# Two transformer blocks on one core: reciprocals, the query's rope and the order of weight splits in latent attention

## The chip, the cores and the metric

The program runs on one core of a Trainium2 chip, as one launch. The metric is the device time in microseconds (us). Engines: TensorE (PE; matmuls and transposes), VectorE (DVE), ScalarE (ACT), GpSimd (POOL) and SyncE (SP), which here issues the weight loads. Each engine works through its own list of instructions in order; semaphores tie the lists together.

## What is computed

256 tokens of width 1024 go through two blocks. In short (`reference`):

```
first_block, layer 0:  x = x + ab_mixer(rms_norm(x))          # mLSTM heads beside a gated mixing, then @ w_out
                       x = x + relu(rms_norm(x) @ w1)**2 @ w2
             layer 1:  x = x + mla_mixer(rms_norm(x))
                       x = x + relu(rms_norm(x) @ w1)**2 @ w2
second_block:          chunked attention with a relative bias, then a SwiGLU, each with norms around it

mla_mixer:  cq, ckv, kr = split(h @ w_in, [384, 640])
            q  = rms_norm(cq) @ w_uq    # 16 heads x (64 without position + 32 rotated)
            kv = rms_norm(ckv) @ w_ukv  # 16 heads x (64 of key + 64 of value)
            rotate the 32 of each query head and the shared kr by position
            p  = softmax(q k^T * 96**-0.5);  out = (p v) @ w_out
apply_rope: [x1 cos - x2 sin, x1 sin + x2 cos]
```

The change concerns the order of the work and the way the rotation is done.

## The kernel before

**Weights and passes.** All matrix products with weights are in full fp32 accuracy by three passes of TensorE: a weight is split into `whi`, a copy rounded to the short format, and `wlo`, the rest; the activations likewise into xh and xl. A product is xh·whi (L373), xl·whi (L374) and xh·wlo (L375), all added in one PSUM tile. `Stream` brings the weights in chunks of up to 1 MB: SP loads a chunk into one of three raw buffers, ACT copies it to `whi` (L149) and DVE, for some chunks POOL, subtracts to get `wlo` (L154), in one, two or four parts; there are four buffers of each. When both halves of a chunk are done with a raw buffer, SP loads the next one. `S.get` hands a chunk to the matmuls, `S.done` lets the coming splits be issued.

**What sets the order.** Within an engine a scheduler sets the order by a timeline it works out; `hot` gives a piece of code priority. Two marks bind the splits of weights: a `wlo` on DVE may not come before the instruction kept in `S.low`, a `whi` on ACT not before the one in `S.behind`. The code sets `S.low` at DVE work that is wanted soon: the copies of qn and kn, the maxima (L1090), the copies of the transposed probabilities, and `split_x` (L302), which splits each finished residual column into xh and xl. `split_x` runs at the end of the mixer (`residual`, L499), of both FFNs (`residual_scaled`, L507, L508) and of the attention.

**Latent attention.** From the input projection (`c_evac`) come the latent ch, cl in two parts. `thin` makes the shared rotary key from the weight wkr, which ACT's queue loads into a place that the first FFN used: DVE scales it (`ws`, L363), TensorE multiplies. `colsum` (L323) adds the squares of the residual on TensorE for the norm; the last sum before it is on DVE (L318). After the values v, `q_rope` makes two of four rotary query tiles: 18 matmuls, a copy to SBUF on ACT (L1000), a shuffle of halves on DVE (L1002), the cosine product on POOL (L1003), the sine product (L1004) and the sum (L1005) on DVE. `q_nope` (18 matmuls, a copy to qn, L1008) and `k_nope` (12 matmuls, kn, L1013) make the rest for one of four groups of four heads. For each group `sc` writes the scores into four PSUM tiles (L1074 for the part without position, L1079 for the rotary part) and `exps` reads them: maxima on DVE (L1089, L1090), eight exponentials on ACT (L1093) that also sum. `nrm` takes reciprocals of the sums (DVE, L1100) and multiplies the probabilities (DVE and POOL, L1103), `tr` transposes them on TensorE (L1117) and copies them to pT (L1122), `pv` multiplies by v (L1132) and splits the result into yh and yl (L1142, L1143), `c_out` is the output projection. TensorE's order in this stage is that of the code. Matmul results rotate through four PSUM tiles (`mm`), scores through four others (`aux`).

## Time and profile before

| | |
|---|---|
| Time, three runs | 898.32, 900.12, 904.68 us; median 900.12 |
| Profiled execution | 897.51 us; its span 895.8 us |
| Busy | TensorE 865.6 us (97%), DVE 573.8 (64%), ACT 469.6 (52%), POOL 268.5 (30%) |
| Mean granted clock of TensorE | 0.990 of full |
| Stages (us of the span) | the mixer's last sums with the residual at 134, the first FFN's at 308, first scores of the attention at 342 |

The profile is of one execution. Its span runs from the first to the last instruction; 1.7 us of the execution's time lie around it. A timeline row gives the start, the duration, the engine, the line of the kernel, the operation and what it writes from what; "x4" means that four like instructions are merged, and the bracket tells how long the engine had been idle before it and what ended the idle. A merged row's duration is that of the whole.

### The profile page before, as it was taken

To read this page: it belongs to the slowest core of one execution; us is meant where nothing else is said; L and a number is where in the kernel's file an instruction comes from. 1 tells how busy PE (TensorE), PEld (TensorE's weight loads), DVE (VectorE), ACT (ScalarE), POOL (GpSimd) and SP (SyncE) were. 2 spreads that over 40 slices of the span, in tenths; PEclk is the share of its full clock that TensorE was granted. 3 is DMA by queue.
4 is the path that set the end of the run, shared out by engine and by line. 5 is a ranking of instruction groups with operands and counts; after the bars stand their busy time and mean duration, and the time that the engine had idled before them with its cause. 6 is when DMAs were issued, how large, how long until landed. Compare 5 with 4: busy or idle time off the path is not lost.

```text
span 895.8 us, 16451 instructions
## 1 busy us (share of the span) xinstructions
PE 865.6 (97%) x6744; PEld 805.2 (90%) x6744; DVE 573.8 (64%) x921; ACT 469.6 (52%) x824; POOL 268.5 (30%) x281
## 2 busy tenths in 40 slices
PE   8899989999999997799999999999999999999996
PEld 6788989999999996589999999999867799999885
DVE  7698768755355658846855456658873776666442
ACT  6676545855444363545655544515476664455331
POOL 6877713333100443375433212320156000000000
PEclk9999999999999999999999999999999999999999
DMA  8543427655455532223755455569424465555511
GB/s 288 215 146 137 141 79 257 218 201 194 142 190 188 194 130 95 95 94 102 277 193 201 170 183 194 190 204 304 154 94 142 165 235 192 194 197 202 185 67 48
DMA packets 25579, 154.38 MB, mean 172 GB/s; under 512 B 2736, under 2 KB 5216, under 8 KB 8224
## 3 DMA queue, kind: packets, MB, share of 16 engines
q1 hardware_dynamic: 22176, 148.18, 46.8%
q10 hardware_dynamic: 3040, 4.36, 2.0%
q8 instruction: 53, 0.87, 0.4%
q0 software_dynamic: 288, 0.79, 0.3%
q14 instruction: 22, 0.18, 0.1%
HBM read 152.25 MB, written 1.07 MB: 171 GB/s over the span
## 4 chain that ended last, share of the span: by engine, by line
PE 83%; DVE 8%; ACT 3%; issue 2%; DMA 2%; POOL 0%; SPq 0%; DVEq 0%; POOLq 0%; ACTq 0%
PE mm L373 20%; PE mm L375 20%; PE mm L374 20%; PE aux L472 2%; PE aux L471 2%; PE aux L470 2%; PE mm L435 2%; DVE acc L717 2%; DVE wlo L154 2%; PE mm L437 2%; PE mm L436 2%; ACT whi L149 1%; ACT pr L1093 1%; PE aux L1074 1%; PE mm L470 1%
## 5 line engine op out<-in xcount | busy, mean ns | idle before, releaser
L149 ACT ACTIVATE whi<-raw 128x1024 fp32r<-128x1024 f32 (+2 forms) x318 | 285.3, 951 | 225.7 <-PE mm L374 140.2
L154 DVE TENSOR_TENSOR wlo<-raw,whi 128x1024 fp32r<-128x1024 f32 (+2 forms) x254 | 307.4, 1251 | 80.1 <-ACT whi L149 80.0
L373 PE MATMUL mm<-xh,whi 128*128 128x256 f32 x1080 | 300.3, 279 | 0.2 <-DVE head L499 0.2
L374 PE MATMUL mm<-xl,whi 128*128 128x256 f32 x1080 | 299.0, 277 | 0.0
L375 PE MATMUL mm<-xh,wlo 128*128 128x256 f32 x1080 | 298.6, 277 | 0.0
L373 PEld LDWEIGHTS mm<-xh,whi 128*128 128x128 f32 x1080 | 203.0, 189 | 1.0 <-issue 0.8
L374 PEld LDWEIGHTS mm<-xl,whi 128*128 128x128 f32 x1080 | 203.6, 189 | 0.2
L375 PEld LDWEIGHTS mm<-xh,wlo 128*128 128x128 f32 x1080 | 203.5, 189 | 0.0
L373 PE MATMUL mm<-hh,whi 128*128 128x256 f32 x512 | 141.3, 276 | 0.0
L374 PE MATMUL mm<-hl,whi 128*128 128x256 f32 x512 | 141.3, 276 | 0.0
L375 PE MATMUL mm<-hh,wlo 128*128 128x256 f32 x512 | 141.3, 276 | 0.0
L373 PEld LDWEIGHTS mm<-hh,whi 128*128 128x128 f32 x512 | 96.1, 188 | 0.0
L374 PEld LDWEIGHTS mm<-hl,whi 128*128 128x128 f32 x512 | 96.1, 188 | 0.0
L375 PEld LDWEIGHTS mm<-hh,wlo 128*128 128x128 f32 x512 | 96.1, 188 | 0.0
L524 POOL TENSOR_TENSOR fu<-ft 128x512 f32<-128x512 f32 (+1 forms) x36 | 55.2, 1536 | 116.5 <-ACT ft L522 111.8
L154 POOL TENSOR_TENSOR wlo<-raw,whi 128x512 fp32r<-128x512 f32 (+2 forms) x64 | 81.8, 1305 | 21.2 <-ACT whi L149 21.1
L318 POOL TENSOR_TENSOR s_acc<-s_acc,sq 128x256 f32<-128x256 f32 x37 | 40.4, 1098 | 147.8 <-ACT sq L317 147.1
L1229 POOL TENSOR_TENSOR r<-v,nhalf 128x1 f32<-128x1 f32 x4 | 2.2, 558 | 193.5 <-DVE v L1228 193.5
L435 PE MATMUL mm<-whi,xh 128*128 128x512 f32 x96 | 38.7, 420 | 1.3 <-ACT whi L149 1.3
L436 PE MATMUL mm<-wlo,xh 128*128 128x512 f32 x96 | 37.9, 398 | 1.7 <-DVE wlo L154 1.7
L437 PE MATMUL mm<-whi,xl 128*128 128x512 f32 x96 | 37.7, 396 | 0.6 <-DVE xl L1438 0.6
L525 DVE TENSOR_TENSOR hl<-fu,hh 128x512 fp32r<-128x512 f32 (+1 forms) x36 | 23.3, 650 | 22.4 <-POOL fu L524 22.4
(371 smaller groups left out, 1314.4 us busy)
## 6 DMA issues: line engine op xcount, KB each, us to landing
raw<-in_w_dram SPq DMA_DIRECT2D x64, 1024.0 KB, 5.0
raw<-in_w_gu_dram SPq DMA_DIRECT2D x22, 1024.0 KB, 4.8
raw<-in_w_qk_dram SPq DMA_DIRECT2D x12, 1024.0 KB, 4.9
raw<-in_w_down_dram SPq DMA_DIRECT2D x11, 1024.0 KB, 4.9
raw<-in_w_ab_out_dram SPq DMA_DIRECT2D x4, 1024.0 KB, 5.0
raw<-in_w_c_out_dram SPq DMA_DIRECT2D x4, 1024.0 KB, 5.1
raw<-in_w_v_dram SPq DMA_DIRECT2D x4, 1024.0 KB, 7.0
raw<-in_w_o_dram SPq DMA_DIRECT2D x4, 1024.0 KB, 4.8
```

The lines of the kernel that those rows point to most:

```text
L149: self.nc.scalar.activation(hi[:, s], r[:, s], AF.Copy)
L154: eng.tensor_tensor(lo[:, s], r[:, s], hi[:, s].bitcast(F32), op=ALU.subtract)
L318: state["sum"] = (dve if k == last else pool).tensor_tensor(acc, acc, sq, op=ALU.add)
L373: pe.matmul(ps, wh, h, start=start, stop=False)
L374: pe.matmul(ps, wh, l, start=False, stop=False)
L375: pe.matmul(ps, wl, h, start=False, stop=stop)
L435: pe.matmul(pss[tt], h[k][:, ts], wh[:, s], start=k == 0, stop=False)
L436: pe.matmul(pss[tt], h[k][:, ts], wl[:, s], start=False, stop=False)
L437: pe.matmul(pss[tt], l[k][:, ts], wh[:, s], start=False, stop=k == nk - 1)
L470: pe.matmul(ps, h[k][:, ts], wh[:, ns], start=k == 0, stop=False)
L524: pool.tensor_tensor(u[:, 0:g], t[:, 0:g], t[:, 0:g], op=ALU.mult)
L525: dve.tensor_tensor(hl[:, m:m + g], u[:, 0:g], hh[:, m:m + g].bitcast(F32), op=ALU.subtract)
```

## The change

It has four parts. `split_x` no longer sets `S.low`; it keeps its instruction aside, and only the end of the attention puts it into `S.low`. The reciprocals are issued after the instruction in `S.low`. In the rotation the ACT copy goes: shuffle and cosine product read PSUM on DVE, the sine product goes to POOL, the sum stays on DVE. The second `q_rope` is moved from ahead of the first `q_nope` to between the first and second group of scores, and with it the points at which chunks are fetched and released; the second half of the query weights is fetched after the second scores. Beside these, the probabilities get 12 buffers instead of 16, and the rest of the output, yl, sets `S.low`.

```diff
--- before.py
+++ after.py
@@ -302,8 +302,8 @@
     def split_x(k, src, scale):
 
         act.activation(xh[:, k], src, AF.Copy, scale=scale)
-        S.low = dve.scalar_tensor_tensor(xl[:, k], src, scale, xh[:, k].bitcast(F32), op0=ALU.mult,
-                                         op1=ALU.subtract)
+        state["xl"] = dve.scalar_tensor_tensor(xl[:, k], src, scale, xh[:, k].bitcast(F32), op0=ALU.mult,
+                                               op1=ALU.subtract)
 
     def split_lo(k, g):
         dve.scalar_tensor_tensor(xl[:, k], x[:, k], col(g, k), xh[:, k].bitcast(F32), op0=ALU.mult,
@@ -909,6 +909,7 @@
         v = ap.tile([P, 2, D], F32, name="v")
         yh, yl = [None] * KB, [None] * KB
         pT_ = [ap.tile([P, 2, T], F32, name=f"pT{i}") for i in range(4)]
+        q2_ = ap.tile([P, 2, T], F32, name="q2")
         mp = mpc.__enter__()
         r2 = ap.tile([P, 2], F32, name="r2")
         rq = ap.tile([P, 2], F32, name="rq")
@@ -996,13 +997,11 @@
 
             ps = tiles(w, 6 * g, CK[2:5], CL[2:5], 3, 2)
             qs = qr[:, 2 * g:2 * g + 2]
-            q2 = mp.tile([P, 2, T], F32, tag="q2", name="q2")
-            act.activation(qs, ps, AF.Copy)
             for i in range(2):
-                dve.stream_shuffle(q2[:, i], qs[:, i], SHUF)
-                pool.tensor_tensor(qs[:, i], qs[:, i], cosT, op=ALU.mult)
-                dve.tensor_tensor(q2[:, i], q2[:, i], sinT, op=ALU.mult)
-                S.low = dve.tensor_tensor(qs[:, i], qs[:, i], q2[:, i], op=ALU.add)
+                dve.stream_shuffle(q2_[:, i], ps[:, i], SHUF)
+                S.low = dve.tensor_tensor(qs[:, i], ps[:, i], cosT, op=ALU.mult)
+                pool.tensor_tensor(q2_[:, i], q2_[:, i], sinT, op=ALU.mult)
+                dve.tensor_tensor(qs[:, i], qs[:, i], q2_[:, i], op=ALU.add)
 
         def q_nope(w, g):
             S.low = dve.tensor_copy(qn[g], tiles(w, 6 * (g % 2), CK[2:5], CL[2:5], 3, 2))
@@ -1051,10 +1050,8 @@
         w = S.get()
         q_rope(w, 0)
         key_rope()
-        q_rope(w, 1)
-        S.done()
-        w = S.get()
-        q_nope(w, 0)
+        wn = S.get()
+        q_nope(wn, 0)
         wk = S.get()
         k_nope(wk, 0)
         later.flush()
@@ -1084,7 +1081,7 @@
             for p in range(2):
                 mx = mp.tile([P, 2, 2], F32, tag="mx", name="mx", bufs=3)
                 sm = mp.tile([P, 2, 2], F32, tag="sm", name="sm", bufs=8)
-                prs = [mp.tile([P, 2, T], F32, tag="pr", name="pr", bufs=16) for _ in range(2)]
+                prs = [mp.tile([P, 2, T], F32, tag="pr", name="pr", bufs=12) for _ in range(2)]
                 for i in range(2):
                     dve.tensor_reduce(mx[:, i], pss[2 * p + i], axis=AX, op=ALU.max)
                 S.low = dve.tensor_tensor(mx, mx, spread(nsrq.unsqueeze(1), 1, 2), op=ALU.mult)
@@ -1097,7 +1094,8 @@
 
         def nrm(j):
             prs, sm = st_p[j]
-            dve.reciprocal(sm, sm)
+            with tc.issue_after(S.low.ins):
+                dve.reciprocal(sm, sm)
             for i in range(2):
                 for qt in range(2):
                     (pool if i else dve).tensor_scalar(prs[i][:, qt], prs[i][:, qt], sm[:, i, qt:qt + 1], None,
@@ -1140,19 +1138,19 @@
                 S.behind = act.activation(yh[j], o[:, 0:T], AF.Copy)
             else:
                 dve.tensor_copy(yh[j], o[:, 0:T])
-            dve.tensor_tensor(yl[j], o[:, 0:T], yh[j].bitcast(F32), op=ALU.subtract)
+            S.low = dve.tensor_tensor(yl[j], o[:, 0:T], yh[j].bitcast(F32), op=ALU.subtract)
 
         sc(0)
-        q_nope(w, 1)
+        q_nope(wn, 1)
+        S.done(held=3)
+        k_nope(wk, 1)
+        q_rope(w, 1)
         S.done(held=2)
-        k_nope(wk, 1)
-        w = S.get()
-        q_nope(w, 2)
         nrm(0)
         nrm(1)
         sc(1)
-        q_nope(w, 3)
-        S.done(held=2)
+        w = S.get()
+        q_nope(w, 2)
         k_nope(wk, 2)
         tr(0)
         tr(1)
@@ -1160,6 +1158,8 @@
         nrm(2)
         nrm(3)
         sc(2)
+        q_nope(w, 3)
+        S.done(held=2)
         k_nope(wk, 3)
         S.done()
         tr(2)
@@ -1201,6 +1201,7 @@
                 for k in (6, 7):
                     c_out(w, m, k)
             hot(residual, 2 * g, pss[g], s_acc[1], "ffn_norm1")
+        S.low = state["xl"]
         S.done(t=5.0)
         mctx.__exit__(None, None, None)
         mpc.__exit__(None, None, None)
```

In the rows of order below a name's number is that of its tile, and the bracket names what the instruction waits for (a load of SP's queues is DMAHW).

DVE at the end of the mixer, in the output projection (L806, L788 make its inputs; L499 adds finished tiles to the residual; wlo_1448 belongs to the last chunk of its weights). Before:

```order
L788 TENSOR_TENSOR yah_1114<-yt_1344,yah_1114 128x256 [waits Activation_49]
L499 TENSOR_TENSOR head_78<-mm_1299,head_78 128x256 [waits PE_49]
L499 TENSOR_TENSOR head_78<-mm_1306,head_78 128x256 [waits PE_49]
L499 TENSOR_TENSOR head_78<-mm_1310,head_78 128x256 [waits PE_49]
L499 TENSOR_TENSOR head_78<-mm_1314,head_78 128x256 [waits PE_49]
L305 SCALAR_TENSOR_TENSOR xl_93<-head_78,xh_92 128x256 [waits DVE_49,Activation_49] x2
L499 TENSOR_TENSOR head_78<-mm_1443,head_78 128x256 [waits PE_49]
L499 TENSOR_TENSOR head_78<-mm_1443,head_78 128x256
L305 SCALAR_TENSOR_TENSOR xl_93<-head_78,xh_92 128x256 [waits DVE_49,Activation_49] x2
L154 TENSOR_TENSOR wlo_1448<-raw_1199,whi_1447 128x1024 [waits DMAHW2_49]
L154 TENSOR_TENSOR wlo_1448<-raw_1199,whi_1447 128x1024
```

With the change, where wlo_1448 stands:

```order
L818 TENSOR_TENSOR sg_158<-mm_1221,rbc0_86 128x512 [waits PE_49]
L788 TENSOR_TENSOR ybl_153<-yt_1187,ybh_152 128x256 [waits Activation_49]
L154 TENSOR_TENSOR wlo_1448<-raw_1199,whi_1447 128x1024 [waits DMAHW2_49,Activation_49]
L806 SCALAR_TENSOR_TENSOR yt_1258<-aux_1255,head_78,sg_158 128x256 [waits DVE_49]
L154 TENSOR_TENSOR wlo_1448<-raw_1199,whi_1447 128x1024 [waits Activation_49]
L788 TENSOR_TENSOR ybl_153<-yt_1210,ybh_152 128x256 [waits Activation_49]
L788 TENSOR_TENSOR yah_1114<-yt_1258,yah_1114 128x256 [waits Activation_49]
L806 SCALAR_TENSOR_TENSOR yt_1272<-aux_1269,head_78,sg_158 128x256 [waits DVE_49]
L806 SCALAR_TENSOR_TENSOR yt_1331<-aux_1328,head_78,sg_158 128x256 [waits DVE_49,PE_49,Pool_49]
```

Both halves of wlo_1448 have moved from behind four xl and six L499 to before the last inputs of the projection; one yt (L806) stands between them, and the last ybl and all the yah (L788) behind them.

DVE at the end of the first FFN, its last column. Before:

```order
L507 TENSOR_TENSOR rs_3620<-mm_3507,rbc0_86 128x256 [waits PE_49]
L508 TENSOR_TENSOR head_78<-rs_3620,head_78 128x256 [waits DVE_49]
L318 TENSOR_TENSOR s_acc0_88<-s_acc0_88,sq_3623 128x256 [waits Activation_49,Pool_49]
L305 SCALAR_TENSOR_TENSOR xl_93<-head_78,xh_92 128x256 [waits DVE_49,Activation_49]
L363 TENSOR_TENSOR ws_3870<-wkr_3659,head_78 128x256 [waits DMAHW1_49]
```

With the change:

```order
L507 TENSOR_TENSOR rs_3620<-mm_3507,rbc0_86 128x256 [waits PE_49]
L508 TENSOR_TENSOR head_78<-rs_3620,head_78 128x256 [waits DVE_49]
L363 TENSOR_TENSOR ws_3871<-wkr_3660,head_78 128x256 [waits DMAHW1_49]
L318 TENSOR_TENSOR s_acc0_88<-s_acc0_88,sq_3623 128x256 [waits Activation_49,Pool_49]
L305 SCALAR_TENSOR_TENSOR xl_93<-head_78,xh_92 128x256 [waits DVE_49,Activation_49]
```

L363, which waits for the load of wkr, has moved ahead of the last sum of squares (L318) and of the last xl (L305).

ACT in the attention, between the values and the second chunk of query weights (whi_4021 before, whi_4092 with the change). Before:

```order
L1025 ACTIVATE v_3644<-mm_3926,rkv_3654 128x512 [waits PE_49]
L149 ACTIVATE whi_4021<-raw_3883 128x768 [waits DMAHW3_49,Pool_49]
L149 ACTIVATE whi_4021<-raw_3883 128x768
L1000 ACTIVATE qr_3642<-mm_3943 128x512 [waits PE_49]
L1000 ACTIVATE qr_3642<-mm_3984 128x512 [waits PE_49]
L1093 ACTIVATE pr_4086,sm_4085<-aux_4064,mx_4084,srq_3655 128x256 [waits DVE_49,DMAHW1_49,PE_49,Pool_49]
L1093 ACTIVATE pr_4086,sm_4085<-aux_4064,mx_4084,srq_3655 128x256
```

With the change (lines are shifted by one to three):

```order
L1024 ACTIVATE v_3644<-mm_3927,rkv_3655 128x512 [waits PE_49]
L1090 ACTIVATE pr_4048,sm_4047<-aux_4026,mx_4046,srq_3656 128x256 [waits DVE_49,DMAHW1_49,PE_49,Pool_49]
L1090 ACTIVATE pr_4048,sm_4047<-aux_4026,mx_4046,srq_3656 128x256
L1090 ACTIVATE pr_4049,sm_4047<-aux_4027,mx_4046,srq_3656 128x256 [waits PE_49]
L1090 ACTIVATE pr_4049,sm_4047<-aux_4027,mx_4046,srq_3656 128x256
L1090 ACTIVATE pr_4059,sm_4058<-aux_4028,mx_4057,srq_3656 128x256 [waits DVE_49,PE_49]
L1090 ACTIVATE pr_4059,sm_4058<-aux_4028,mx_4057,srq_3656 128x256
L1090 ACTIVATE pr_4060,sm_4058<-aux_4029,mx_4057,srq_3656 128x256 [waits PE_49]
L1090 ACTIVATE pr_4060,sm_4058<-aux_4029,mx_4057,srq_3656 128x256
L149 ACTIVATE whi_4092<-raw_3884 128x768 [waits DMAHW3_49,Activation_49]
L149 ACTIVATE whi_4092<-raw_3884 128x768
```

The copies qr are gone, and the two whi of the second query chunk have moved from ahead of the first group's exponentials to behind them.

DVE from there, behind the first group's maxima. Before:

```order
L1090 TENSOR_TENSOR mx_4084<-mx_4084,nsrq_3656 128x4 [waits DVE_49]
L1090 TENSOR_TENSOR mx_4095<-mx_4095,nsrq_3656 128x4 [waits DVE_49]
L1100 RECIPROCAL sm_4085<-sm_4085 128x4 [waits Activation_49]
L1008 COPY qn_3635<-mm_4106 128x512 [waits PE_49]
L1103 TENSOR_SCALAR pr_4086<-pr_4086,sm_4085 128x256 [waits DVE_49]
L1103 TENSOR_SCALAR pr_4086<-pr_4086,sm_4085 128x256
L1013 TENSOR_TENSOR kn_3639<-mm_4126,rbc1_87 128x256 [waits PE_49]
L1013 TENSOR_TENSOR kn_3639<-mm_4126,rbc1_87 128x256
L1100 RECIPROCAL sm_4096<-sm_4096 128x4 [waits Activation_49]
L1103 TENSOR_SCALAR pr_4097<-pr_4097,sm_4096 128x256 [waits DVE_49]
L1103 TENSOR_SCALAR pr_4097<-pr_4097,sm_4096 128x256
L154 TENSOR_TENSOR wlo_4131<-raw_3923,whi_4130 128x1024 [waits DMAHW4_49,Activation_49]
```

With the change:

```order
L1007 COPY qn_3635<-mm_4068 128x512 [waits PE_49]
L1012 TENSOR_TENSOR kn_3639<-mm_4088,rbc1_87 128x256 [waits PE_49]
L1012 TENSOR_TENSOR kn_3639<-mm_4088,rbc1_87 128x256
L154 TENSOR_TENSOR wlo_4093<-raw_3884,whi_4092 128x768 [waits DMAHW3_49,Activation_49]
L1001 STREAM_SHUFFLE q2_3649<-mm_4106 128x256 [waits PE_49]
L1002 TENSOR_TENSOR qr_3642<-mm_4106,cosT_96 128x256
L1001 STREAM_SHUFFLE q2_3649<-mm_4106 128x256
L1002 TENSOR_TENSOR qr_3642<-mm_4106,cosT_96 128x256
L1098 RECIPROCAL sm_4047<-sm_4047 128x4
L1098 RECIPROCAL sm_4058<-sm_4058 128x4
L154 TENSOR_TENSOR wlo_4093<-raw_3884,whi_4092 128x768 [waits Activation_49]
L154 TENSOR_TENSOR wlo_4169<-raw_3924,whi_4168 128x1024 [waits DMAHW4_49,Activation_49]
```

The reciprocals have moved behind the copies qn and kn of the second group, behind half a split of the second query chunk, which waits for ACT, and behind four instructions of the second rope half.

## Rows read from the trace of the kernel before

**Rows 1.** Waits of TensorE over the span: us in total, times, longest.
```profile
PE aux L1074 <- DVE kn L1013: 4.8, 2, 3.5
PE mm L375 <- DVE wlo L154: 2.4, 1, 2.4
```

**Rows 2.** Windows: us; busy us (instructions) of each engine; clock; DMA share; GB/s.
```profile
127.00:130.40 3.40, 3.40 (x17) 3.40 (x18) 3.40 (x5) 0.00 (x0) 0.00 (x0) 0.50 0.40 87
342.60:345.70 3.10, 3.10 (x16) 2.45 (x16) 3.10 (x5) 0.00 (x0) 0.00 (x0) 0.54 0.03 5
365.40:369.50 4.10, 4.10 (x18) 2.46 (x20) 4.10 (x8) 1.76 (x2) 1.82 (x2) 0.58 0.00 0
390.00:420.00 30.00, 30.00 (x255) 27.36 (x254) 12.76 (x27) 19.50 (x42) 21.29 (x20) 1.00 0.32 106
```

**Rows 3.** Timeline of TensorE, end of the mixer: start, us, ..., [idle before <-releaser].
```profile
110.62 0.28 PE L374 MATMUL mm<-ybl,whi 128*128 128x256 f32 x1
...
126.89 0.48 PE L375 MATMUL mm<-yah,wlo 128*128 128x256 f32 x1 [2.43 <-DVE wlo L154]
```

**Rows 4.** Timeline of DVE, end of the mixer.
```profile
107.44 0.48 DVE L806 SCALAR_TENSOR_TENSOR yt<-aux,head,sg 128x256 f32<-128x256 f32 x1
109.11 0.42 DVE L788 TENSOR_TENSOR ybl<-yt,ybh 128x256 fp32r<-128x256 f32 x1 [1.19 <-ACT ybh L787]
...
125.09 2.88 DVE L154 TENSOR_TENSOR wlo<-raw,whi 128x1024 fp32r<-128x1024 f32 x2
```

**Rows 5.** Timeline of ACT, end of the mixer.
```profile
106.78 1.99 ACT L149 ACTIVATE whi<-raw 128x1024 fp32r<-128x1024 f32 x2
```

**Rows 6.** Timeline of DVE, end of the first FFN.
```profile
310.62 1.55 DVE L318 TENSOR_TENSOR s_acc<-s_acc,sq 128x256 f32<-128x256 f32 x1 [1.14 <-ACT sq L317]
...
314.73 0.42 DVE L363 TENSOR_TENSOR ws<-wkr,head 128x256 f32<-128x256 f32 x1 [1.14 <-DMA wkr<-in_w_ckr_dram]
```

**Rows 7.** Timeline of TensorE, last matmul of the FFN and the projection behind.
```profile
308.28 0.28 PE L375 MATMUL mm<-hh,wlo 128*128 128x256 f32 x1
...
312.82 0.50 PE L323 MATMUL aux<-ones,s_acc 128*128 128x1 f32 x4
```

**Rows 8.** DMA issues by line: count, KB each, us to landing.
```profile
wg<-in_w_gates_dram POOLq DMA_DIRECT2D x1, 128.0 KB, 4.1
...
wkr<-in_w_ckr_dram ACTq DMA_DIRECT2D x1, 128.0 KB, 6.1
```

**Rows 9.** Timeline of TensorE, attention.
```profile
342.57 3.41 PE L1074 MATMUL aux<-kn,qn 64*128 64x256 f32 x16 [3.50 <-DVE kn L1013]
...
354.02 2.00 PE L1074 MATMUL aux<-kn,qn 64*128 64x256 f32 x16 [1.31 <-DVE kn L1013]
...
363.92 0.65 PE L1117 MATMUL mm<-ident,pr 128*128 128x128 f32 x4 [2.22 <-DVE qn L1008]
365.33 0.63 PE L1117 MATMUL mm<-ident,pr 128*128 128x128 f32 x4 [0.75 <-POOL pr L1103]
...
377.62 1.31 PE L1117 MATMUL mm<-ident,pr 128*128 128x128 f32 x8 [2.22 <-DVE kn L1013]
```

**Rows 10.** Timeline of DVE, attention.
```profile
333.64 0.42 DVE L977 TENSOR_TENSOR kr<-aux,rbc 128x256 f32<-128x256 f32 x1
...
335.85 0.86 DVE L980 TENSOR_TENSOR k<-k,sinT 128x256 f32<-128x256 f32 x1
...
338.19 0.41 DVE L1005 TENSOR_TENSOR qr<-qr,q 128x256 f32<-128x256 f32 x1
...
340.83 0.68 DVE L1008 COPY qn<-mm 128x512 f32<-128x512 f32 x1
...
347.07 2.48 DVE L1089 TENSOR_REDUCE mx<-aux 128x2 f32<-128x512 f32 x4 [1.03 <-PE aux L1079]
...
352.13 0.18 DVE L1100 RECIPROCAL sm<-sm 128x4 f32<-128x4 f32 x1 [2.37 <-ACT pr L1093]
...
355.29 1.21 DVE L154 TENSOR_TENSOR wlo<-raw,whi 128x1024 fp32r<-128x1024 f32 x1
...
385.90 0.42 DVE L1143 TENSOR_TENSOR yl<-mm,yh 128x256 fp32r<-128x256 f32 x1
```

**Rows 11.** Timeline of ACT, attention.
```profile
349.80 0.56 ACT L1093 ACTIVATE pr<-aux,mx,srq 128x256 f32<-128x256 f32 x1 [13.49 <-DVE mx L1090]
...
354.15 2.02 ACT L149 ACTIVATE whi<-raw 128x1024 fp32r<-128x1024 f32 x2
```

**Rows 12.** Timeline of POOL, attention.
```profile
335.69 1.62 POOL L1003 TENSOR_TENSOR qr<-qr,cosT 128x256 f32<-128x256 f32 x2 [0.32 <-DVE q L1002]
```

## The prediction

> **What bounds the kernel now.** I read the busy shares first: TensorE works 97% of the span, so only two things can be won, its idle time and the stretches at the lower clock. Its waits come next [rows 1]: away from the start the largest are 4.8 us for kn in the latent attention and 2.4 for the last weight split of the mixer's output projection. The windows then show what an idle costs behind itself [rows 2]: in full work 255 matmuls take 30.00 us, 0.118 each, at clock 1.00; three stretches stand at 0.50 to 0.58, the lower level (1.2 of 2.4 GHz). The first gives the clean price: 3.40 us at 0.50 do the work of 1.70, so 1.7 us are lost. They follow idles of 2.43 [rows 3], of 3.50, and of 2.22 with a shorter one before the next work; a lone idle of 2.22 before 377.62 and one of 1.31 before 354.02 were followed by full clock [rows 9]. So I charge 1.7 extra to an idle of about 2.5 us or more and nothing to one of 2.2 or less. Attention from 339 to 386 idles 3.50, 1.31, 2.22 and 2.22 there, with one of 0.75 more 10.0 us; with two slow stretches it loses 13.4.
>
> **End of the mixer: the x splits no longer hold back weight splits.** Before, both halves of the split wlo_1448 stood on DVE behind four residual x splits; they began at 125.09, and TensorE got what it needed at 126.89 [rows 3, 4]. ACT had their whi by 106.78 + 1.99 = 108.8 [rows 5]. Now they stand either side of the small yt product that ran at 107.44, so they run at 107.9 to 110.7 (2.88 for two [rows 4]). Behind them ybl, which ran at 109.11 [rows 4], is done at about 111.0. TensorE reached its matmul at 110.62 [rows 3], so 0.4 us goes there. Gone are 2.43 idle and 1.7 of clock: 4.1 less 0.4, a gain of **3.7**. Bounds: 2.0 (the clock falls all the same) and 4.1. Where does the stall go next? The following splits move forward too, DVE has nothing else until it adds the first finished tiles, and FFN0 behind it ran without an idle: nothing is late there.
>
> **End of the first FFN: the same edit, another order.** `ws`, which waits for the load of wkr, now stands ahead of the residual's sum of squares and of xl. Before, DVE did the sum at 310.62 and only later waited for wkr, until 314.73 [rows 6]; TensorE took the sum at 312.82 [rows 7]. The load took 6.1 us [rows 8], so it was issued at 308.6, when the FFN's last matmul freed its place [rows 7]. With that landing, ws and the sum (0.42 each when nothing runs beside them, as ws did) follow: sum at 315.5, TensorE idles 2.7 us, and the clock falls (1.7): a loss of 4.4. The other weight load of that size landed in 4.1 us [rows 8]: sum at 313.6, idle 0.8. Before, a load of 768 KB was issued beside wkr; with splits done and buffers free earlier there is less beside it now. I take 5 us: sum at 314.4, idle 1.6, clock kept: **loss 1.5**, bounds 0.8 and 4.4.
>
> The Trainium skill (SBUF — State Buffer, "The DMA setup-cost knee") puts any transfer at some 2 us plus its bytes over 436 GB/s; by that estimate wkr is there 2.3 us after its issue and the loss is 0. The trace does not agree: 6.1 and 4.1 were measured.
>
> **Attention, in the times of before.** (1) Eighteen matmuls of the second rope half, 2.1 us, leave the front: k_nope(0) ends at 337.0, not 342.57 − 3.50 = 339.07. (2) DVE does from 333.64 some nine small operations (0.41 each, 0.34 behind one another), a qn copy (0.68), one wlo half (1.21) and two kn: kn(0) at 339.0, not 342.57 [rows 9, 10]. Idle 2.0 instead of 3.5, and the clock stays. (3) So sc(0) begins 3.6 earlier and takes 2.00 where it took 3.41 [rows 9]: it ends at 342.1, before at 347.07, where the maxima start [rows 10]. (4) Maxima 2.48 and 0.3: the exponentials start at 344.9 (before 349.80) and take 4.4 [rows 11]: 349.3. (5) 48 matmuls (nope 18, k 12, rope 18) fill 342.1 to 347.7; sc(1) waits 0.7 for PSUM that the exponentials free and ends at 351.4. (6) The change does **less than its name says**: the reciprocal no longer blocks DVE first (2.37 us before [rows 10]), but a wlo of uq2 now does, because its whi on ACT has moved behind the exponentials: 346.3 to 350.2. (7) Behind it: wlo 0.9, four rope operations 1.4, reciprocals 0.3, two wlo 2.2, the first product 0.4: tr(0) at 355.5. (8) tr(1) waits for PSUM, that is for the qn and kn copies of group 2, which stand on DVE behind the maxima of sc(1): 360.2, idle 3.5 (before 2.22 and 0.8), clock falls; pv(0) 362 to 364. (9) Exponentials of group 1 end at 364.0, of group 2 at 375.2; sc(3) runs 375 to 378. (10) The lead is lost again: on DVE the pT copies, the wlo of c_out that waited for ACT, reciprocals, products and maxima stand before the last yl. pv(3) waits until 380.8 (idle 2.7, clock falls); the fourth c_out tile, which needs that yl, comes at 386.0 to 386.3, before at 385.90 + 0.42 [rows 10]. Idle is about 11 instead of 10.0, and two slow stretches again. **Net −0.2**, with bounds −3 (the idles of (8) and (10) stay below what costs clock) and +5.8 (rival C).
>
> The two qr copies on ACT go (1.2 us): ACT is idle there, worth nothing. The sine products move from DVE to POOL, hidden behind the qn matmuls. Loads of c_out move up on SP by some us; no matmul waited for a load. With 12 pr buffers for 16 the last group of exponentials takes those of the first, which TensorE has transposed by 361: no wait.
>
> **Rows against a rule.** The k sine product took 0.86 on DVE while POOL ran two cosine products, a like operation 0.41 afterwards [rows 10, 12]; the sum at 310.62 took 1.55 [rows 6]. The Trainium skill (SBUF — State Buffer, "Who interferes with whom") has DVE operations with two SBUF inputs and reading GpSimd ones take a shared port pair in turn. These rows agree, and the rule speaks against handing POOL more.
>
> **Sum.** −3.7 + 1.5 − 0.2 = −2.4 us on the profiled execution's 897.51: 895.1. That execution lies 2.6 below the median, so the median becomes **897.7**.
>
> **Rivals.** (A) *wkr lands late, 6.1 us again, and the clock falls:* 4.4 instead of 1.5, 900.6. For it stands the load's own row; against it, less traffic. (B) *wkr is no stall and attention's idles stay short:* −3.7 + 0 − 3, 893.4. For it: step (4) is 5 us early; against: 4.1 is the shortest such landing shown. (C) *Slower: POOL and DVE in each other's way in attention.* Sine products, the products of L1101 and wlo halves are new neighbours; eight wlo halves at 1.44 (half of 2.88) for 1.21 cost 1.8, and nine two-input operations at 0.86 for 0.41 another 4.0, together 5.8 on the DVE chain of (2) to (10), which paces the stage: 897.7 + 5.8 = 903.5. From 2.4 us on the whole gain is eaten; against it, most such operations now read PSUM on one side. With A it is 906.
>
> **Numbers.** Forecast 0.45, A 0.17, B 0.20, C 0.18. The range, 890 to 904, reaches from B with both gains at their bounds to C without A. A median tells some 1% (9 us) from no change. Faster than 891 takes B and an attention that gains 5 rather than 3 (0.12). Slower than 909 takes C, A and the mixer's lower bound, −2.0 + 4.4 + 5.8 on 900.1, and a little more (0.07). The rest, 0.81, lies within.
>
> **What would show it.** TensorE without the 2.4 us wait at 126.9 and without the slow stretch behind it; a new wait for the sum at 312.8 (none: B); kn's wait 2.0 instead of 3.5 and sc(0) at full clock; DVE idle before uq2's wlo, ended by ACT; tr(1) waiting 3.5 for qn or kn. I am wrong if attention idles under 8 or over 14 us, or if waits appear in the FFNs or behind attention.

## The result: slower by 0.8%, outside the range

| | before | after the change |
|---|---|---|
| Median of nine runs (lowest to highest) | 898.51 us (897.14 to 904.68) | 906.67 us (903.91 to 908.51) |
| Ratio, 95% interval | | 1.0081 [1.0065, 1.0097] |
| Profiled execution, its span | 897.51, 895.8 us | 906.24, 904.5 us |
| Mean granted clock | 0.990 | 0.991 |

The forecast was 897.7 us with a range of 890 to 904. The sign of the small difference was wrong, and the time lies above the range. The mean clock is not lower than before, so clock alone can't be where the time went.

I laid the two traces over each other at fixed points of the program. The second column says by how much the change is later there than before, the third what that stage added.

| Point (us in the trace of before) | change later by | stage added | predicted |
|---|---|---|---|
| Mixer's ybl products (105.5) | +2.02 | +2.0 | 0 |
| Norm sum of the first FFN (144.1) | −1.83 | **−3.9** | −3.7 |
| End of the first FFN (308.3) | +3.83 | **+5.7** | 0 |
| Norm sum behind it (312.8) | +4.81 | **+1.0** | +1.5 |
| Values (323.6) | +4.60 | −0.2 | 0 |
| Last pv of the attention (382.9) | +2.2 | **−2.4** | −2.1 |
| Transposes inside the output projection (390.1) | +8.70 | **+6.5** | +1.9 |
| End of the span | +8.7 | 0 | 0 |

Of the +2.0 at the start, 1.6 arise between 72 and 77 us, where the two kernels issue the same instructions; the other kernels, with the same code up to there, stood at −0.8 to +2.2. I count it as chance. The two stages to explain are the first FFN and the tail of the attention.

**Waits of TensorE after the change** (us in total, times, longest), largest first:

```profile
PE mm L373 <- DVE yl L1141: 4.7, 1, 4.7
PE mm L1115 <- DVE qn L1007: 3.5, 1, 3.5
PE aux L1071 <- DVE kn L1012: 2.2, 1, 2.2
...
PE mm L1130 <- DVE pT L1120: 1.3, 1, 1.3
...
```

Both waits of [rows 1] have gone or shrunk: wlo at the end of the mixer is no longer there, kn has 2.2 where one of its two was 3.5. In their place stand 4.7 for the last yl and 3.5 for qn. No wait at all stands for the 5.7 us of the FFN.

**End of the mixer.** Timeline of DVE after the change, the rows that answer to [rows 4]:

```profile
109.87 1.23 DVE L154 TENSOR_TENSOR wlo<-raw,whi 128x1024 fp32r<-128x1024 f32 x1 [0.46 <-ACT whi L149]
111.01 0.48 DVE L806 SCALAR_TENSOR_TENSOR yt<-aux,head,sg 128x256 f32<-128x256 f32 x1
111.41 1.22 DVE L154 TENSOR_TENSOR wlo<-raw,whi 128x1024 fp32r<-128x1024 f32 x1
112.54 0.83 DVE L788 TENSOR_TENSOR ybl<-yt,ybh 128x256 fp32r<-128x256 f32 x1
```

TensorE's only wait there, and the window that follows (us; busy time and instructions of PE, PEld, DVE, ACT, POOL; clock; DMA share; GB/s):

```profile
113.42 0.38 PE L374 MATMUL mm<-ybl,whi 128*128 128x256 f32 x1 [0.62 <-DVE ybl L788]
...
115.00:131.00 16.00, 16.00 (x138) 16.00 (x138) 12.83 (x20) 10.47 (x19) 5.96 (x5) 1.00 0.48 182
```

The two halves stand either side of yt, ybl comes behind them, TensorE waits 0.6 for it (0.4 was predicted), and the clock is 1.00 where [rows 2] had 0.50. This step is right.

**The first FFN.** Two windows over the same 140 us, the first after the change, the second before it:

```profile
160.00:300.00 140.00, 140.00 (x1191) 140.00 (x1191) 78.03 (x82) 67.51 (x86) 29.45 (x17) 1.00 0.55 190
```

```profile
160.00:300.00 140.00, 140.00 (x1237) 140.00 (x1237) 78.81 (x86) 74.72 (x99) 27.19 (x18) 1.00 0.55 192
```

TensorE is busy all the time in both, at full clock, on the same kind of matmul, and finishes 1191 in one and 1237 in the other: a **pitch of 0.1176 us against 0.1132**. Over the some 1,360 matmuls from 152 to 312 us that makes 1,360 × 0.0044 = 6.0; the stage lost 5.7. (The expectations below count from start to start, 0.1178 and 0.1133; a window also counts the matmuls that reach over its edges.) So the engine works at two paces that neither the waits nor the clock show. In this stage the slower one begins at one place, which the timeline of TensorE after the change shows; L347 spreads the norm's factor over the partitions by a product of `dg` and ones, in two matmuls:

```profile
151.93 0.40 PE L347 MATMUL aux<-dg,ones_r 128*128 128x256 f32 x2
152.17 0.28 PE L373 MATMUL mm<-xh,whi 128*128 128x256 f32 x1
```

Before the change the two stood apart:

```profile
153.76 0.28 PE L347 MATMUL aux<-dg,ones_r 128*128 128x256 f32 x1
...
155.51 0.39 PE L347 MATMUL aux<-dg,ones_r 128*128 128x256 f32 x1
```

Up to 151.8 three matmuls take 0.34 us, from 152.17 on 0.35; the slow pace holds up to the sum L323 at 317.63, ahead of which TensorE stands still for 0.65 us.

The kernel before has the slow pace too, in another place. Ahead of the four sum matmuls L323 at 312.82 [rows 7] the matmuls stand 0.1133 apart; behind them, with no idle and with no L347 near, 46 of them take 5.43 us, 0.118 each:

```profile
313.39 0.28 PE L374 MATMUL mm<-xl,whi 128*128 128x256 f32 x1
...
318.81 0.28 PE L375 MATMUL mm<-xh,wlo 128*128 128x256 f32 x1
```

**Input projection.** Timeline of DVE after the change, answering to [rows 6]:

```profile
316.11 1.14 DVE L363 TENSOR_TENSOR ws<-wkr,head 128x256 f32<-128x256 f32 x1 [2.80 <-DMA wkr<-in_w_ckr_dram]
317.17 0.41 DVE L318 TENSOR_TENSOR s_acc<-s_acc,sq 128x256 f32<-128x256 f32 x1
```

TensorE, and the load itself (KB, us to landing):

```profile
317.63 0.61 PE L323 MATMUL aux<-ones,s_acc 128*128 128x1 f32 x4 [0.65 <-DVE s_acc L318]
```

```profile
wkr<-in_w_ckr_dram ACTq DMA_DIRECT2D x1, 128.0 KB, 3.6
```

The wait is the predicted one; the load took 3.6 where I had taken 5, but ws took 1.14 where it took 0.42 in [rows 6]. It ended 0.3 us behind the last of three subtractions of POOL, which ended at 316.96:

```profile
313.07 3.89 POOL L154 TENSOR_TENSOR wlo<-raw,whi 128x512 fp32r<-128x512 f32 x3 [3.04 <-ACT whi L149]
```

**Attention.** Timeline of TensorE after the change, answering to [rows 9]:

```profile
343.96 2.00 PE L1071 MATMUL aux<-kn,qn 64*128 64x256 f32 x16 [2.21 <-DVE kn L1012]
...
365.67 1.84 PE L1115 MATMUL mm<-ident,pr 128*128 128x128 f32 x8 [3.48 <-DVE qn L1007]
...
385.11 1.68 PE L1130 MATMUL mm<-pT,v 128*64 128x256 f32 x8 [1.32 <-DVE pT L1120]
...
393.70 0.55 PE L373 MATMUL mm<-yh,whi 128*128 128x256 f32 x1 [4.66 <-DVE yl L1141]
...
398.79 1.04 PE L1115 MATMUL aux<-ident,pr 128*128 128x128 f32 x8
```

The attention starts 4.6 later than before, so 4.6 is to be taken off. The last pv then stands at 380.5 (predicted 380.8), the fourth output tile at 389.1 (predicted 386.0 to 386.3). Behind it the clock falls:

```profile
393.70:397.00 3.30, 3.30 (x15) 3.30 (x16) 1.41 (x5) 3.30 (x14) 2.14 (x3) 0.50 0.00 0
```

What DVE did ahead of that last yl, with an earlier group of the same products (372.57) for comparison:

```profile
372.57 1.77 DVE L1101 TENSOR_SCALAR pr<-pr,sm 128x256 f32<-128x256 f32 x4
...
381.76 2.36 DVE L154 TENSOR_TENSOR wlo<-raw,whi 128x1024 fp32r<-128x1024 f32 x2 [2.29 <-ACT whi L149]
...
386.56 0.23 DVE L1098 RECIPROCAL sm<-sm 128x4 f32<-128x4 f32 x2
386.76 3.34 DVE L1101 TENSOR_SCALAR pr<-pr,sm 128x256 f32<-128x256 f32 x4
390.02 1.87 DVE L1086 TENSOR_REDUCE mx<-aux 128x2 f32<-128x512 f32 x3
...
393.13 0.42 DVE L1141 TENSOR_TENSOR yl<-mm,yh 128x256 fp32r<-128x256 f32 x1
```

And POOL in the same stretch:

```profile
383.27 5.75 POOL L154 TENSOR_TENSOR wlo<-raw,whi 128x512 fp32r<-128x512 f32 x4 [6.82 <-ACT whi L149]
389.00 3.68 POOL L1101 TENSOR_SCALAR pr<-pr,sm 128x256 f32<-128x256 f32 x4
```

The four products of DVE take 3.34 here and 1.77 at 372.57, where POOL runs its own products beside them and no weight split: 1.6 us on the chain that ends in the last yl. The first two products and the two splits beside them, one by one:

```profile
386.76 1.11 DVE L1101 TENSOR_SCALAR pr<-pr,sm 128x256 f32<-128x256 f32 x1
387.79 1.37 DVE L1101 TENSOR_SCALAR pr<-pr,sm 128x256 f32<-128x256 f32 x1
...
386.44 1.28 POOL L154 TENSOR_TENSOR wlo<-raw,whi 128x512 fp32r<-128x512 f32 x1
387.68 1.34 POOL L154 TENSOR_TENSOR wlo<-raw,whi 128x512 fp32r<-128x512 f32 x1
```

Each of the two ends 0.15 us behind a subtraction of POOL (387.87 behind 387.72, 389.16 behind 389.02). The first product at 372.57, which began ahead of POOL's, took 0.35.

### The profile page after: what moved, and what is told of

The parts are those of the page before. It is cut to its first block, busy times and chain, and to the rows that moved or that the text cites. A ratio compares the mean times of both kernels' runs of the same rounds, so it can differ in the third digit from the quotient of the medians.

```text
span 904.5 us, 16488 instructions
## 1 busy us (share of the span) xinstructions
PE 872.8 (96%) x6744; PEld 811.6 (90%) x6744; DVE 573.5 (63%) x921; ACT 468.5 (52%) x822; POOL 270.1 (30%) x281
## 4 chain that ended last, share of the span: by engine, by line
PE 81%; DVE 9%; ACT 3%; issue 3%; DMA 2%; POOL 1%; SPq 0%; DVEq 0%; POOLq 0%; ACTq 0%
PE mm L373 20%; PE mm L374 20%; PE mm L375 20%; PE aux L471 2%; PE aux L470 2%; PE aux L472 2%; DVE wlo L154 2%; DVE acc L717 2%; PE mm L435 2%; PE mm L437 2%; PE mm L436 2%; ACT whi L149 1%; PE mm L470 1%; DMA raw<-in_w_qk_dram 1%; ACT pr L1090 1%
## 5 line engine op out<-in xcount | busy, mean ns | idle before, releaser
L149 ACT ACTIVATE whi<-raw 128x1024 fp32r<-128x1024 f32 (+2 forms) x318 | 285.0, 951 | 229.2 <-PE mm L374 144.1
L154 DVE TENSOR_TENSOR wlo<-raw,whi 128x1024 fp32r<-128x1024 f32 (+2 forms) x254 | 302.2, 1227 | 126.7 <-ACT whi L149 125.1
L318 POOL TENSOR_TENSOR s_acc<-s_acc,sq 128x256 f32<-128x256 f32 x37 | 41.7, 1133 | 152.4 <-ACT sq L317 141.9
```

Source lines behind the costliest of these rows:

```text
L149: self.nc.scalar.activation(hi[:, s], r[:, s], AF.Copy)
L154: eng.tensor_tensor(lo[:, s], r[:, s], hi[:, s].bitcast(F32), op=ALU.subtract)
L318: state["sum"] = (dve if k == last else pool).tensor_tensor(acc, acc, sq, op=ALU.add)
```

## The experiments

Two theories for the FFN: the pace follows from **the two L347 matmuls standing back to back** (the rhythm theory), or from the new order of DVE and ACT work, which the same edit brings (the order theory). A third is that it falls by chance in each execution. For the tail: the **reciprocals and products queued ahead of the last yl**, **POOL in DVE's way**, or **wlo late because ACT makes its whi late**.

### Each half of the change alone

`split_only` is the kernel before with the edit of `split_x`; `attention_only` is the change without it.

```diff
 # split_only, against before
-        S.low = dve.scalar_tensor_tensor(xl[:, k], ...)
+        state["xl"] = dve.scalar_tensor_tensor(xl[:, k], ...)
...
+        S.low = state["xl"]      # end of the attention
```

> The edit of the x splits alone, the attention as before. Two theories of where the change's loss in the first FFN (+5.7 us from the sum matmuls at its start to its last matmul) comes from. Rhythm theory: the two broadcast matmuls L347 now run back to back, no wait between them, and leave TensorE in a slower rhythm (0.1178 us a matmul instead of 0.1133, both at clock 1.00) until its next wait. Order theory: the other order of weight splits beside the FFN slows the matmuls. Both expect here: mixer -3.9, first FFN +5.7 at 0.1178 a matmul, input projection +1.0, attention within 0.5 of before: 2.8 us slower than before. A third theory, that the rhythm falls by chance in each run, expects either 2.8 slower or 2.9 faster.

> All of the change but the edit of the x splits, which hold splits back again. Both theories of the FFN: its matmuls at 0.1133 again, the 2.4 us wait at the mixer's end back, no wait for the load of wkr ahead of the sum. Tail theory of the attention (its lead of 3.8 us at sc(3) is lost where the wlo of c_out, four products and the maxima stand before the last yl): a wait of 4 to 5 us for yl in c_out and the low clock behind it, attention 4.1 us longer, the kernel 4 us slower than before. If the attention had only lost to the slower start behind the FFN, it would be within 1 us of before.

Measured: `split_only` 902.65, ratio 1.0015 [0.9994, 1.0036]; `attention_only` 903.41, 1.0039 [1.0008, 1.0070]. In its profile `split_only` gains 3.9 in the mixer and loses 5.7 in the FFN (pair back to back at 150.06, 1191 matmuls in the window) and 2.7 in the attention; `attention_only` has the fast pace (1238) and loses 3.3 in the attention. So the FFN's loss belongs to the edit of `split_x`, and a loss in the attention is there without it. The 2.7 of `split_only` are more than the expected 0.5; how far such a figure of one profile can be read is said below. The ten times of `split_only`, 901.25 to 905.28, lie within 4.0 us, less than the 5.7 between the two paces: they give no sign that the pace changes from execution to execution where the pair stands together.

### The pair moved apart in the change, and together in the kernel before

The scheduler's due time for the two matmuls decides where they stand; nothing else is edited.

```diff
 # change_early_spread, against the change
-                bcast(rbc[0], r_col[1], dt=5.0)
+                bcast(rbc[0], r_col[1], dt=2.0)
 # before_late_spread, against before
+                bcast(rbc[0], r_col[1], dt=8.0)
```

> The change, with the two broadcast matmuls L347 of the FFNs asked for earlier (2 instead of 5 steps after their diagonals), so that in the first FFN they are apart again and the second waits for its diagonal. Rhythm theory: matmuls at 0.1133 behind the wait, first FFN 5.4 us shorter than in the change (5.7 less a wait of 0.3): 901.3 where the change has 906.7. Order theory: the splits stand as in the change, 0.1178, within 0.5 us of the change.

> The kernel before, with the two broadcast matmuls L347 of the FFNs asked for later (8 instead of 5 steps), so that they stand back to back with no wait. Rhythm theory: 0.1178 a matmul from there to the next wait, first FFN 5.7 us longer, the kernel 5.7 slower than before (if the second FFN's pair does the same, 11). Order theory: 0.1133, within 0.5 us of before.

Measured: `change_early_spread` 902.51, 1.0025 [0.9995, 1.0056]; `before_late_spread` 910.39, 1.0098 [1.0067, 1.0128]. In the latter both FFNs have the pair back to back, and both run slowly. Its timeline and windows:

```profile
158.19 0.40 PE L347 MATMUL aux<-dg,ones_r 128*128 128x256 f32 x2
...
447.18 0.40 PE L347 MATMUL aux<-dg,ones_r 128*128 128x256 f32 x2
...
160.00:300.00 140.00, 140.00 (x1191) 140.00 (x1191) 77.81 (x88) 72.67 (x94) 26.07 (x17) 1.00 0.52 182
460.00:600.00 140.00, 140.00 (x1191) 140.00 (x1190) 78.14 (x80) 68.94 (x92) 39.11 (x23) 1.00 0.50 174
```

The x splits hold back weight splits here as they did before, and the two FFNs still lose 5.5 and 6.2 us: the order theory falls. With the pair apart the change's FFN has 1237 matmuls in the window again; TensorE's order in that stage differs from the change's by the pair alone, and a few instructions of DVE and ACT move with it.

### The tail: reciprocals undone, whi freed, both, and the reciprocals alone

```diff
 # change_plain_recip, against change_early_spread
-            with tc.issue_after(S.low.ins):
-                dve.reciprocal(sm, sm)
+            dve.reciprocal(sm, sm)
 # change_free_whi, against change_early_spread: exponentials of the third group don't hold back whi
-                        S.behind = act.activation(...)
+                        e = act.activation(...)
+                        if a != 2:
+                            S.behind = e
 # change_both: both edits.  before_recip_only, against before, in the attentions of both blocks:
+            with tc.issue_after(S.low.ins):
```

> As change_early_spread, with the reciprocals not held behind S.low. Two theories of the attention's tail (in the change pv(3) waits 1.3 and the fourth c_out tile 4.7 us for its yl). Products theory: the reciprocals' move brings two of them and four products (0.2 + 3.3 us on DVE) between the last pT copies and the last yl; without it they run during the exponentials, the wait for yl falls to about 1 us and the clock stays: 3.5 + 1.7 less, from which the reciprocals' own blocking takes 1 to 2 back, so the stretch from the values to the first transposes within c_out is 3 us shorter than in change_early_spread. Splits theory: what counts are the two wlo of c_out that wait for ACT (idle 2.3, work 2.4): within 1 us of change_early_spread.

> As change_early_spread, with the weight copies on ACT not held behind the third group's exponentials, so that the whi of c_out's second chunk stand ahead of them. Splits theory: DVE's idle of 2.3 us before their wlo goes, pv(3) and the last yl come 2.3 earlier, and if the wait for yl falls near 2 the clock stays: 2.3 to 4 us shorter from the values to the transposes within c_out than change_early_spread. Products theory: the exponentials start up to 1.6 later behind the copies, the products as late: within 1 us of change_early_spread.

> Both: plain reciprocals and free weight copies. Products theory: 3 us shorter than change_early_spread as with the reciprocals alone. Splits theory: 2.3 to 4. If both add: about 6, attention then 2 to 3 us shorter than in the kernel before, the kernel 5 to 6 us faster than before with the mixer's gain.

> The kernel before with only the reciprocals held behind S.low. Products theory: reciprocals and products now stand between the pT copies and the last yl of each pair here too, so the tail waits for yl: 3 to 5 us slower than before. Splits theory: the wlo stand early as before, no new wait: 0 to 2 us faster, since the 2.4 us for which a reciprocal blocked DVE go to other work.

Measured, the ratio to before on the same chip, and how much longer the attention (values to the transposes of the output projection) is than before in the profile:

| Kernel | median, us | ratio [95%] | attention |
|---|---|---|---|
| the change (first result) | 906.67 | 1.0081 [1.0065, 1.0097] | +4.1 |
| change_early_spread | 902.51 | 1.0025 [0.9995, 1.0056] | +5.6 |
| change_plain_recip | 907.95 | 1.0070 [1.0035, 1.0105] | +5.2 |
| change_free_whi | 903.20 | 1.0015 [0.9985, 1.0045] | +4.5 |
| change_both | 905.22 | 1.0059 [1.0030, 1.0089] | +8.0 |
| before_recip_only | 900.67 | 1.0015 [0.9982, 1.0048] | +4.5 |

The last column is of one profile each and carries some noise: `before_late_spread`, whose DVE and POOL have the order of before in the attention, stands at +1.8. `split_only`, `mixer_only` and `mixer_early_spread` (the last two below), edited ahead of the attention, stand at +2.7, +1.3 and +1.7, and there the scheduler has also moved DVE instructions of the attention. Differences below some 2 us are not read here. The reciprocals alone, put into the kernel before, lose as much there as the whole change. DVE of `before_recip_only`:

```profile
379.43 0.36 DVE L1101 RECIPROCAL sm<-sm 128x4 f32<-128x4 f32 x2
...
380.54 4.89 DVE L1104 TENSOR_SCALAR pr<-pr,sm 128x256 f32<-128x256 f32 x4
385.36 0.41 DVE L1144 TENSOR_TENSOR yl<-mm,yh 128x256 fp32r<-128x256 f32 x1
```

Its TensorE waits 2.57 for the last yl, at 389.43. But its median does not move by a resolved amount, and taking the same edit out of the change (`change_plain_recip`) did not make the attention shorter: the wait for yl falls from 4.7 to 2.5, where the products theory had about 1, but waits for kn (2.4 and 1.1) and for qn (1.6) come in its place. There the reciprocals wait for the exponentials at the head of DVE's list again, and the weight split falls into POOL's; DVE of `change_both`, to be read against the 2.36 above:

```profile
377.66 3.95 DVE L154 TENSOR_TENSOR wlo<-raw,whi 128x1024 fp32r<-128x1024 f32 x2
```

So each edit shortens its own wait, and others on the same engine take its place. The theory that one of the two edits holds the loss failed.

### POOL out of DVE's way, and another chunk for POOL

`change_pool_free` has ACT write the low part of one output chunk, as zeros, where POOL subtracted; that low part is left out of the computation. `change_swap_chunk` gives POOL the second chunk in place of the third.

```diff
 # change_pool_free, against the change
+                if i == self.plain:     # third chunk of w_c_out
+                    self.nc.scalar.activation(lo[:, s], r[:, s], AF.Copy, scale=0.0)
+                else:
+                    eng.tensor_tensor(lo[:, s], r[:, s], ...)
 # change_swap_chunk, against change_early_spread
-  "w_c_out": (2, 3)
+  "w_c_out": (1, 3)
```

> The change, with the low halves of c_out's third weight chunk made by ACT as a copy times zero instead of POOL's subtraction (so its low part is left out of the product); DVE's order is that of the change. Contention theory: the four products of probabilities before the last yl took 3.3 us because POOL subtracted weights beside them; without that 1.7, the last yl 1.6 earlier, the wait for it 3.1 instead of 4.7 us. If POOL has no part in it: 3.3 and 4.7 as in the change.

> As change_early_spread, with c_out's second chunk split by POOL and its third by DVE. Splits theory of the tail: DVE no longer waits 2.3 us for ACT ahead of two wlo of 2.4, pv(3) and the last yl come up to 4.7 earlier, less what the products lose beside POOL: the wait for yl falls from 4.7 to between 1 and 3 and the clock stays, 3 to 5 us from the values to the transposes within c_out. Products theory: the products stay ahead of the last yl, 0 to 2 us.

Measured: `change_pool_free` 905.04, 1.0037 [1.0010, 1.0064]; `change_swap_chunk` 904.97, 1.0026 [0.9991, 1.0061]. With POOL's subtraction gone (POOL runs its own products there, from 386.54 on, as it does beside those at 372.57), DVE's products and TensorE's wait in `change_pool_free`:

```profile
386.41 1.77 DVE L1107 TENSOR_SCALAR pr<-pr,sm 128x256 f32<-128x256 f32 x4
```

```profile
391.78 0.36 PE L379 MATMUL mm<-yh,whi 128*128 128x256 f32 x1 [3.10 <-DVE yl L1147]
```

The products take 1.77 instead of 3.34, and the wait for yl falls by the same 1.6, from 4.66 to 3.10. That POOL's splits slow DVE's products, and that this is 1.6 us of the tail, is shown. The attention as a whole is not shorter for it in this profile, +4.3 against +4.1, because its first scores ran at the low clock, 3.68 us where the change has 2.00 (see the price of an idle, below). The swap only moved the waiting: yl 4.47, pT 2.26, attention +6.5.

### The mixer's part alone

`mixer_only` keeps `S.low` back in the mixer's `residual` only; `mixer_early_spread` adds dt=2.0.

```diff
 # mixer_only, against before, in residual
+            low = S.low
             split_x(k, x[:, k], col(g, k))
+            if g == "ffn_norm0":
+                S.low = low
```

> The kernel before, with S.low left alone only by the x splits of the mixer's output projection; FFNs and attention hold splits back as before, so wkr is waited for after the sum. L347's pair stands back to back in the first FFN. Rhythm theory: mixer -3.9, first FFN +5.7 at 0.1178 a matmul, attention as before: 1.8 slower than before. Order theory of the FFN (the splits in it are what slows it; they stand as before here): 0.1133 and 3.9 faster.

> As mixer_only, with L347 asked for after 2 steps instead of 5, which sets the pair apart with a wait for the second. Rhythm theory: mixer -3.9, first FFN at 0.1133, input projection and attention as before: 3.7 us faster than before, 0.4%, and so faster than both kernels. Order theory: the same as mixer_only.

Measured: `mixer_only` 902.49, 1.0014 [0.9989, 1.0040], pair back to back, 1191 in the window; `mixer_early_spread` 897.48, 0.9984 [0.9952, 1.0015]. The latter's timeline and window:

```profile
148.81 0.28 PE L347 MATMUL aux<-dg,ones_r 128*128 128x256 f32 x1
...
150.77 0.28 PE L347 MATMUL aux<-dg,ones_r 128*128 128x256 f32 x1
...
160.00:300.00 140.00, 140.00 (x1238) 140.00 (x1237) 76.73 (x85) 70.67 (x90) 25.93 (x18) 1.00 0.54 190
```

The same edit in the mixer, nearly the same order of the splits, and the pace changes with the place of the pair. This kernel has the lowest median of all (897.48 against 899.87 of the kernel before on that chip), but the interval holds 1: it is not shown to be faster. Its profile is 0.4 us shorter than that of before: +1.9 at the start, −3.8 in the mixer, −0.35 in the first FFN, +1.7 in the attention. Its twelve times fall into two groups, seven from 895.55 to 897.84 and five from 902.49 to 904.40. That the upper group had the slow pace would fit; only one execution was profiled, so it is not shown.

### What holds over all profiles

In the FFNs the back-to-back pair was followed by the slow pace in all six stretches that had it (first FFN of the change, `split_only`, `mixer_only`, `change_pool_free` and `before_late_spread`, and the second FFN of the last). With the pair apart, eight of nine first FFNs and all 13 second ones were fast. The exception is `change_swap_chunk`: its two are 1.9 us apart, and the slow pace runs from there on all the same (1191 in the window). In this stage it has the very order of `change_early_spread` on all four engines, and that one ran fast: the order of the program alone does not decide.

```profile
146.56 0.28 PE L347 MATMUL aux<-dg,ones_r 128*128 128x256 f32 x1
...
148.50 0.37 PE L347 MATMUL aux<-dg,ones_r 128*128 128x256 f32 x1
```

Outside the FFNs the pair is no sure sign. In the input projection two L347 stand back to back in all 14 kernels; three matmuls later four sum matmuls follow, and behind those the pace was fast in ten profiles and slow in four (before, `change_early_spread`, `change_plain_recip`, `mixer_early_spread`), which had been slow ahead of the pair already. The slow pace also begins without a pair (before, at 312.82 above), ends without a standstill (`before_late_spread`, at the sum matmuls at 319.90 and 611.71), and outlasts one (0.49 us in `change_pool_free`, at 315.38). Every change of pace that the profiles show from the first FFN's sum to the end of the second FFN's, attention apart, lies within a microsecond of matmuls of another kind put between; most such interruptions change nothing.

So moving the pair together brings the slow pace on in these FFNs, but standing apart does not exclude it, and the pair is one of several things that can start it. **What in TensorE makes the difference stays open.**

## Why the prediction was wrong, point by point

**Where the 11.1 us between forecast and profile come from.** Forecast −2.4, profile +8.7. Of the difference, +2.0 is the chance at the start, +5.7 the first FFN, −0.7 the projection and the values, −0.2 the mixer, +4.3 the attention.

**Mixer: right.** −3.9 for −3.7, by the steps given: splits forward, 0.6 for ybl, clock kept.

**First FFN: the step that failed.** It read "FFN0 behind it ran without an idle: nothing is late there". I took a stage that TensorE fills to 100% at full clock as one that can't become longer. Nothing became late there, that much holds; the pitch changed. I took the 0.118 of [rows 2] for the price of a matmul in full work. That window is no measure of it: 64 of its matmuls are transposes and products with v, of other shapes, and both paces occur among the rest. But the trace had the possibility in it: the first FFN ran at 0.1132 and the projection behind it at 0.118 (313.39 to 318.81, above), one kind of matmul, one clock, two prices. Moving x splits moved the pair of L347 together, which the order of TensorE's instructions would have shown; I read only DVE's and ACT's there.

**Input projection: mechanism right, size within the bounds.** +1.0 where I took 1.5 between 0.8 and 4.4. The stall went where the step said, to the sum behind `ws`. The load landed in 3.6 us, under the two that I had as bounds; over the 14 profiles it took 2.1 to 6.2. I had priced ws at 0.42, and beside POOL's subtraction it took 1.14. Rival A (6.1 again) did not happen; nor did B's "no stall", not even where the load landed in 2.1 us (`split_only` and `change_pool_free`, where TensorE waited 0.49).

**Attention up to the last pv: right but for one wait.** In times of before: sc(0) 3.2 earlier (3.6 predicted), kn's wait 2.21 (2.0) at full clock, uq2's wlo on DVE ended by ACT at 350.4 (350.2), tr(1)'s wait for qn 3.48 (3.5), pv(3) at 380.5 (380.8). The idle ahead of pv(3) was 1.32 and not 2.7, since sc(3) ran later (376.1 to 379.2 for 375 to 378), and the clock stood at 1.00 behind it where step (10) let it fall.

**Tail: the other step that failed**, "(10) ... the fourth c_out tile ... at 386.0 to 386.3". It came at 389.1. I had named what stands on DVE ahead of the last yl, but priced it too low: from the start of pv(3) to that tile it took 8.6 us where I had 5.2 to 5.5. Of the some 3.2 more, 1.6 are the products beside POOL, as `change_pool_free` shows. The other 1.6 I can't give to one operation: DVE stands still for no more than some 0.04 us at a time from 381.76 up to that yl, and the step gives no price for each operation; this stays open. TensorE's wait grew to 4.66, and the clock fell behind it: the next 15 matmuls took 3.30 us, where 15 × 0.113 = 1.7 is their price at full clock, so another 1.6 are lost.

**Rival C had the mechanism and the wrong place.** It gave POOL and DVE 5.8 us over all of the attention. They did meet at other places, but the kernel before has the like there (sine products of 0.96 and 0.94 for 0.41 at 336.63 and 339.97, beside POOL's cosine products); new is the tail, 1.6 with what the clock adds. The Trainium skill (SBUF — State Buffer, "Who interferes with whom") counts `tensor_scalar` among the operations that can take the port pair shared with GpSimd, and lets the second comer wait until the first is done. The trace agrees: the two products beside POOL's splits took 1.11 and 1.37 and ended 0.15 behind them, the one that began ahead of POOL's work 0.35. I had argued from operations with two SBUF inputs only.

**The price of an idle.** "Nothing to one of 2.2 or less" held in the change, but by luck. The same idle before the same matmuls in `change_both` and in `change_pool_free`:

```profile
335.48 3.44 PE L1071 MATMUL aux<-kn,qn 64*128 64x256 f32 x16 [2.23 <-DVE kn L1012]
```

```profile
341.88 3.68 PE L1077 MATMUL aux<-kn,qn 64*128 64x256 f32 x16 [2.21 <-DVE kn L1018]
```

3.44 and 3.68 for what took 2.00 after 2.21 in the change: an idle of 2.2 us falls on either side. The other half of the rule, 1.7 for 2.5 us or more, has an exception too: in `mixer_early_spread` the same matmuls took 2.00, at clock 1.00, after 3.45.

```profile
340.34 2.00 PE L1077 MATMUL aux<-kn,qn 64*128 64x256 f32 x16 [3.45 <-DVE kn L1016]
```

I should have given either idle a price between 0 and 1.7.

**The signs that I had named did not show the failure.** Those of the forecast came: no 2.4 us wait at the mixer's end, a wait for the sum, kn's wait with sc(0) at full clock, the idle before uq2's wlo, the wait of tr(1). Those of being wrong did not: the attention idled 12.7 us, within 8 to 14, and no wait appeared in the FFNs. Nearly all of these signs are waits, and the largest loss of time is not a wait.

**Open:** why the pace differs; why the medians of `change_plain_recip` and `change_both` lie 6.3 and 3.6 above their own profiled executions (901.68 and 901.67), so that the table of the attention speaks of those executions and not of the medians.

## What to carry to other kernels

A stage in which TensorE is 100% busy at full clock can still have two speeds: divide a window's time by its matmuls, in windows that hold one kind of matmul only, before calling one of them full work, and look at what an edit on another engine does to TensorE's own order. When reciprocals and products are moved to spare one copy, list everything that then stands ahead of the last consumer on that engine, and price each operation with the neighbour that it will have on POOL.

## What the runs showed of the hardware that I had not expected

- TensorE at granted clock 1.00, busy without a gap, on 128×128 by 128×256 fp32 matmuls, keeps one of two paces over 140 us and more: 0.1132 or 0.1176 us a matmul. Two L347 matmuls back to back in an FFN were followed by the slow one in six of six stretches, two apart in one of 22; the slow pace also began at four sum matmuls without a pair (312.82 in the kernel before).
- A `tensor_scalar` of DVE with one tensor input in SBUF took 0.35 us when it began ahead of POOL's work, 1.11 and 1.37 while POOL subtracted in SBUF, ending 0.15 behind POOL's instruction.
- After the same idle of 2.21 to 2.23 us the first 16 score matmuls took 2.00 us in three of the profiles (the change, `change_plain_recip`, `attention_only`), 2.76 in `change_swap_chunk` and 3.2 to 3.7 in four (`change_early_spread`, `change_both`, `change_free_whi`, `change_pool_free`). After 3.45 us they took 2.00 in `mixer_early_spread`.
